# Padded float32 scores, paired latent values and a 128-row decay in a two-layer hybrid decoder

## The chip, the cores and the metric

The kernel runs on one core of one Trainium2 chip. The metric is the device time of one execution in microseconds; smaller is better. All tensors are float32, the sequence has 512 tokens, the model width is 1024.

## The reference

Two layers. Layer 0 mixes tokens by two kinds of attention side by side, layer 1 by two recurrences side by side; after each mixer comes a SwiGLU feed-forward net. What the change touches is this:

```python
# layer 0, latent attention: 8 heads, q and k of 64 + 32 columns, v of 64
o_mla  = softmax(causal(q_mla @ k_mla.T * 96**-0.5)) @ v_mla
# layer 0, differential attention: 4 heads, each with 2 halves of 64 columns
dq, dk = rope(dq), rope(dk)
o2     = softmax(causal(dq @ dk.T * 64**-0.5)) @ dv      # per half, dv has 128 columns
o_diff = rms_norm(o2[half 0] - lam * o2[half 1], subln) * (1 - lambda_init)
# layer 1, state-space group: 8 heads, chunks of 128 tokens
a      = dt * -exp(a_log)
a_cs   = cumsum(a, within the chunk)
seg    = exp(where(causal, a_cs[l] - a_cs[s], -inf))
y_diag = (cc @ bc.T * seg) @ xh
```

## The kernel before, in words

Activations lie feature-major: 128 features on the partitions, 512 tokens in the free dimension. A projection in full precision is split in a high and a low part in a reduced float32 format (`F32R`) and takes three matmuls for each 128 rows of the contraction (`mm3`, L330 to L332). Weights come by SyncE's queue in `wr` tiles (L271) and are split into `wh` and `wl` (L292, L294); pieces 16 to 71 get their lower part on GpSimd, the others on VectorE. At most eight split pieces stand ready (`NSPL`).

Order of work: `attention_layer` first makes the rotary projections of head 0 and the values `dv` of the differential attention; then `weave` runs two generators against each other by hand-written costs: the main one is `diff_attention`, then `latent_attention`, and the filler is all the projections that are left (`diff_projections`, `latent_projections`, `keys`, `queries`, the output projection). The framework under it orders the instructions of each engine and sets the waits. The tiles named `slot` come from one common ring of 37 buffers of 128 x 512, those named `tmp` from one of 10, both are given out again when their last reader is through; PSUM banks `at` are four, `mm` three, `o` one.

Differential attention. `rotary` takes a projection of 128 rows (two halves of 64), turns it (`turn`: two products on VectorE, a sum on GpSimd into `o`) and splits it (`parts`). The queries of a head become three tiles: `t0` and `t1` hold the high part of half 0 and 1 in their own 64 rows and in the other 64 rows a second copy of it; `low` holds what is left. The keys become two tiles: for each half the high part in its own rows and its remainder in the other rows. A score of half c and row block i (`score`, 128 rows, n = 128 (i+1) columns) is then three matmuls: one over 128 rows (L803), the causal mask in bf16 (L804), one over the 64 rows of `low` (L805). `softmax` takes the maximum on VectorE (L708) and the exponential on ScalarE (L710). The two halves are scaled and joined on VectorE (L833, L834) to `p`, which TensorE transposes (L718); the transposes are copied out (L721, L723) and multiplied with `dv` (L821).

Latent attention. The scores are plain float32 matmuls over 128 rows (L701, L702), which the compiler issues as two instructions each, and the mask (L703). The values `v` are four tiles of 128 tokens x 512 columns, 64 columns a head. The product for head h (L867) uses 64 columns of the array and writes PSUM partitions 0 to 63 for an even head, 64 to 127 for an odd one; when both are through, the pair is split once.

State-space group. `ssd` computes dt for 32 columns (four chunks, eight heads), `av` = -dt exp(a_log) (L1073), its running sums as eight rows (`acs`, L1079, L1082), their split, the last sums (L1087, L1091) and their transposes (L1090). In `decay`, for each of eight heads, a row of the selector `sel` spreads one of the eight rows over 128 partitions: two matmuls over 8 rows (L1129, L1131) with the mask between (L1130).

## Time and profile before

| what | value |
|---|---|
| three runs | 1314.17, 1314.99 (median), 1318.85 us |
| profiled execution | 1314.82 us |
| span of its instructions | 1313.0 us |
| TensorE busy | 97% of the span, 6013 matmuls |
| VectorE busy | 56% |
| ScalarE busy | 42% |
| GpSimd busy | 23% |
| mean granted TensorE clock | 0.994 |

The time of the profiled execution is 1.8 us longer than the span from its first to its last instruction. PE is TensorE's matmuls, PEld its weight loads, DVE VectorE, ACT ScalarE, POOL GpSimd, SPq the queue of SyncE. The start of a matmul is measured, its end is modelled, and so neighbouring matmuls overlap in the profile; how long one really holds the engine is read from the distance to the next start. A float32 matmul over full tiles stands in the profile as two instructions. A few matmul records can be missing.

### The profile page before, as it was taken

What the parts mean: (1) busy time and instruction counts of PE and PEld (TensorE: products, weight loads), DVE (VectorE), ACT (ScalarE), POOL (GpSimd) and SP (SyncE); (2) the same over time, 40 slices, a digit from 0 to 9 for tenths busy, and PEclk for the clock granted to TensorE, in tenths of its full rate; (3) what the DMA queues carried; (4) which work ended last, traced back from release to release, by engine and by line L of the source; (5) the groups of instructions that cost most, each with busy time, mean ns of one, the idle gap of its engine ahead of it and who ended that gap; (6) DMA issues with size and microseconds to landing.
All of it is one profiled execution on the core that took longest, in us unless ns stands there. A gap on an engine that the chain in (4) does not pass through costs nothing.

```text
span 1313.0 us, 16410 instructions
## 1 busy us (share of the span) xinstructions
PE 1274.8 (97%) x6013; PEld 1029.9 (78%) x6013; DVE 732.2 (56%) x1330; ACT 545.5 (42%) x1075; POOL 308.2 (23%) x244
## 2 busy tenths in 40 slices
PE   7998889999999999999999999999999999999997
PEld 5766667778888888888888877787788888888886
DVE  6888885557444334444457456799854433344332
ACT  5556554445333223333443463654543322333341
POOL 2524432127222002222100003221322210122212
PEclk9999999999999999999999999999999999999999
DMA  7211211113322333222323321122233223332221
GB/s 236 101 64 33 85 60 49 42 54 112 98 87 82 105 112 97 97 83 89 118 80 97 115 78 33 34 67 62 67 111 97 82 90 118 97 96 87 83 73 64
DMA packets 37135, 112.75 MB, mean 86 GB/s; under 512 B 4272, under 2 KB 10800, under 8 KB 37056
## 3 DMA queue, kind: packets, MB, share of 16 engines
q1 hardware_dynamic: 37056, 111.72, 27.1%
q8 instruction: 47, 0.77, 0.2%
q14 instruction: 32, 0.26, 0.1%
HBM read 109.61 MB, written 2.10 MB: 85 GB/s over the span
## 4 chain that ended last, share of the span: by engine, by line
PE 83%; DVE 10%; ACT 2%; issue 1%; DMA 1%; POOL 1%; SPq 0%; POOLq 0%; DVEq 0%; ACTq 0%
PE mm L330 24%; PE mm L331 24%; PE mm L332 24%; PE o L867 2%; PE at L718 1%; DVE wl L294 1%; PE at L1337 1%; DVE xl L451 1%; PE at L701 1%; DVE nm L708 1%; DMA x<-in_x_dram 0%; PE at L702 0%; DMA par<-in_par_dram 0%; PE at L332 0%; PE at L330 0%
## 5 line engine op out<-in xcount | busy, mean ns | idle before, releaser
L294 DVE TENSOR_TENSOR wl<-wr,wh 128x512 fp32r<-128x512 f32 (+1 forms) x352 | 272.8, 777 | 312.2 <-ACT wh L292 310.1
L292 ACT CAST wh<-wr 128x512 fp32r<-128x512 f32 (+1 forms) x401 | 243.3, 610 | 452.4 <-PE mm L331 398.1
L330 PE MATMUL mm<-xh,wh 128*128 128x512 f32 x944 | 375.7, 398 | 7.1 <-ACT wh L292 6.3
L331 PE MATMUL mm<-xl,wh 128*128 128x512 f32 x944 | 370.9, 393 | 4.2 <-DVE xl L451 4.2
L332 PE MATMUL mm<-xh,wl 128*128 128x512 f32 x944 | 371.2, 393 | 0.0
L330 PEld LDWEIGHTS mm<-xh,wh 128*128 128x128 f32 x944 | 178.8, 189 | 48.4 <-ACT wh L292 6.3
L331 PEld LDWEIGHTS mm<-xl,wh 128*128 128x128 f32 x944 | 178.5, 189 | 42.5 <-DVE xl L451 6.7
L332 PEld LDWEIGHTS mm<-xh,wl 128*128 128x128 f32 x944 | 178.5, 189 | 37.1 <-DVE wl L294 0.4
L929 POOL TENSOR_TENSOR uu<-uu,g 128x512 f32<-128x512 f32 x44 | 70.2, 1598 | 432.8 <-DVE uu L928 408.7
L330 PE MATMUL mm<-hh,wh 128*128 128x512 f32 (+1 forms) x363 | 139.1, 383 | 0.0
L332 PE MATMUL mm<-hh,wl 128*128 128x512 f32 (+1 forms) x363 | 138.9, 383 | 0.0
L331 PE MATMUL mm<-hl,wh 128*128 128x512 f32 (+1 forms) x363 | 138.9, 383 | 0.0
L294 POOL TENSOR_TENSOR wl<-wr,wh 128x512 fp32r<-128x512 f32 (+1 forms) x54 | 70.1, 1303 | 147.4 <-ACT wh L292 147.4
L331 PEld LDWEIGHTS mm<-hl,wh 128*128 128x128 f32 x363 | 68.2, 188 | 13.4
L330 PEld LDWEIGHTS mm<-hh,wh 128*128 128x128 f32 x363 | 68.2, 188 | 13.3
L332 PEld LDWEIGHTS mm<-hh,wl 128*128 128x128 f32 x363 | 68.2, 188 | 13.2
L462 POOL TENSOR_TENSOR acc<-acc,sq 128x512 f32<-128x512 f32 x31 | 45.2, 1457 | 117.4 <-ACT sq L461 116.5
L928 DVE TENSOR_TENSOR uu<-mm,row 128x512 f32<-128x512 f32 x42 | 29.0, 691 | 65.7 <-PE mm L332 65.7
L931 POOL TENSOR_TENSOR hl<-uu,hh 128x512 fp32r<-128x512 f32 x44 | 56.5, 1287 | 29.2 <-ACT hh L930 29.2
L930 ACT CAST hh<-uu 128x512 fp32r<-128x512 f32 x44 | 27.3, 620 | 86.4 <-POOL uu L929 86.4
L710 ACT ACTIVATE p<-at,nm 128x128 f32<-128x128 f32 (+3 forms) x64 | 33.6, 526 | 50.0 <-DVE nm L708 46.5
L954 DVE TENSOR_TENSOR x<-x,mm 128x512 f32<-128x512 f32 x31 | 21.3, 687 | 36.3 <-PE mm L332 36.3
(416 smaller groups left out, 1711.7 us busy)
## 6 DMA issues: line engine op xcount, KB each, us to landing
wr<-in_w_gu_dram SPq DMA_DIRECT2D x88, 512.0 KB, 3.8
wr<-in_w_down_dram SPq DMA_DIRECT2D x32, 512.0 KB, 3.5
wr<-in_w_in_dram SPq DMA_DIRECT2D x20, 512.0 KB, 3.8
wr<-in_w_out_dram SPq DMA_DIRECT2D x12, 512.0 KB, 3.8
wr<-in_w_down_dram SPq DMA_DIRECT2D x32, 192.0 KB, 2.4
wr<-in_w_dv_dram SPq DMA_DIRECT2D x4, 512.0 KB, 4.4
tab<-in_con_dram SPq DMA_DIRECT2D x8, 256.0 KB, 4.3
wr<-in_w_z_dram SPq DMA_DIRECT2D x4, 512.0 KB, 3.6
```

The lines of the kernel that those rows point to most:

```text
L292: nc.scalar.copy(out=hi, in_=raw)
L294: (nc.gpsimd if PL[0] <= self.cut < PL[1] else nc.vector).tensor_tensor(out=lo, in0=raw, in1=hi.bitcast(F32), op=ALU.subtract)
L330: mm(out, lh, rh, start=start, stop=False)
L331: mm(out, lh, rl, start=False, stop=False)
L332: mm(out, ll, rh, start=False, stop=stop)
L462: (nc.vector if fast else nc.gpsimd).tensor_tensor(out=acc, in0=acc, in1=t, op=ALU.add)
L710: nc.scalar.activation(out=pt[:, 0:n], in_=s[:, 0:n], func=AF.Exp, bias=nm, accum_out=rsum)
L867: nc.tensor.matmul(ops[c0 : c0 + 64, vi * P : vi * P + P], self.v[j][:, vh * 64 : (vh + 1) * 64], pT[:, j * P : (j + 1) * P], start=j == 0 ...
L928: nc.vector.tensor_tensor(out=u, in0=pu, in1=row, op=ALU.mult)
L929: nc.gpsimd.tensor_tensor(out=u, in0=u, in1=g, op=ALU.mult)
L930: nc.scalar.copy(out=h, in_=u)
L931: nc.gpsimd.tensor_tensor(out=lo, in0=u, in1=h.bitcast(F32), op=ALU.subtract)
```

## The change

Three edits.

- Differential scores: the keys are no longer split; the sum of `turn` goes straight into a slot. The queries of each half get a tile of their own in plain float32, with zeros in the 64 rows of the other half. A score is one float32 matmul over 128 rows and the mask. A head takes three slots and not five.
- Latent values: `v` is kept in eight tiles. Each holds for two pairs of heads 64 columns of the even head, 64 zeros, 64 columns of the odd head. The product takes two neighbouring groups, so 128 columns: values and zeros for an even head, zeros and values for an odd one, and writes all 128 partitions; both heads of a pair add into the same bank.
- State-space decay: `av` repeats the eight heads sixteen times, so that the running sums, their split, the transposes and the selector all have 128 rows. The selector is loaded with its 128 rows, of which one holds ones.

```diff
--- before.py
+++ after.py
@@ -574,30 +574,26 @@
         u, sw, o = self.tmp("du"), self.tmp("dsw"), self.tmp("dqk")
         nc.scalar.activation(out=u, in_=ps, func=AF.Identity, scale=1.0 if c else 64.0 ** -0.5)
         nc.vector.stream_shuffle(out=sw, in_=u, mask=HALVES)
-
-        t0, t1 = self.slot("d0", F32R), self.slot("d1", F32R)
         a, b = slice(0, 64), slice(64, P)
-        copy, sub = nc.vector.tensor_copy, lambda out, x, hi: nc.vector.tensor_tensor(out=out, in0=x, in1=hi.bitcast(F32), op=ALU.subtract)
 
         def turn():
             nc.vector.tensor_tensor(out=o, in0=u, in1=self.dtab[0], op=ALU.mult)
             nc.vector.tensor_tensor(out=sw, in0=sw, in1=self.dtab[1], op=ALU.mult)
-            nc.gpsimd.tensor_tensor(out=o, in0=o, in1=sw, op=ALU.add)
+            if c:
+                self.dqk[h, 1] = self.slot("dk")
+                nc.gpsimd.tensor_tensor(out=self.dqk[h, 1], in0=o, in1=sw, op=ALU.add)
+            else:
+                nc.gpsimd.tensor_tensor(out=o, in0=o, in1=sw, op=ALU.add)
 
         def parts():
-            nc.scalar.copy(out=t0[a], in_=o[a])
-            nc.scalar.copy(out=t1[b], in_=o[b])
-            if c:
-                sub(t0[b], o[a], t0[a])
-                sub(t1[a], o[b], t1[b])
-                self.dqk[h, 1] = t0, t1
-            else:
-                low = self.slot("dlow", F32R)
-                copy(out=t0[b], in_=o[a])
-                copy(out=t1[a], in_=o[b])
-                sub(low[a], o[a], t0[a])
-                sub(low[b], o[b], t1[b])
-                self.dqk[h, 0] = t0, t1, low
+
+            if c == 0:
+                t0, t1 = self.slot("dq0"), self.slot("dq1")
+                nc.gpsimd.memset(t0[b], 0.0)
+                nc.gpsimd.memset(t1[a], 0.0)
+                nc.scalar.copy(out=t0[a], in_=o[a])
+                nc.scalar.copy(out=t1[b], in_=o[b])
+                self.dqk[h, 0] = t0, t1
 
         self.defer(R0, turn)
         self.defer(R1, parts)
@@ -615,7 +611,11 @@
         ckh, ckl = [self.slot("ckh", F32R) for _ in range(2)], [self.slot("ckl", F32R) for _ in range(2)]
         accq, acck, kr = self.slot("accq"), self.slot("acck"), self.slot("kr")
         self.ck, self.cq = (ckh, ckl), (cqh, cql)
-        self.v = [self.slot("v") for _ in range(4)]
+
+        self.v = [[self.slot("v")[:, 0:384].rearrange("p (g t f) -> p g t f", t=3, f=64) for _ in range(2)] for _ in range(4)]
+        for b in range(NB):
+            for j in range(2):
+                nc.gpsimd.memset(self.v[b][j][:, :, 1, :], 0.0)
         own = {}
 
         def scale_kv():
@@ -664,8 +664,14 @@
                 else:
                     self.square_into(accq, ps, j == 3)
                     self.split(cqh[j - 3], cql[j - 3], ps, par[:, C_QN + j - 3 : C_QN + j - 2])
+
+        def values(b, ps):
+            for j in range(2):
+                src = ps[:, 256 * j : 256 * j + 256].rearrange("p (g t f) -> p g t f", g=2, t=2)
+                nc.scalar.activation(out=self.v[b][j][:, :, 0::2, :], in_=src, func=AF.Identity, scale=own["sk"][:, b : b + 1])
+
         yield from hooked(
-            self.tokmajor4("uv", ckh, ckl, lambda b, ps: nc.scalar.activation(out=self.v[b], in_=ps, func=AF.Identity, scale=own["sk"][:, b : b + 1])),
+            self.tokmajor4("uv", ckh, ckl, values),
             {SQ[0]: scale_q, SQ[1]: spread_q},
         )
         yield from self.keys(0)
@@ -791,18 +797,15 @@
             n = (i + 1) * P
             if t < 16:
                 if i == 0:
-                    yield lambda: (h, 1) in self.dqk
+                    yield lambda: (h, 0) in self.dqk and (h, 1) in self.dqk
                 rs, ri = self.small(2, "rs2", bufs=4), self.small(2, "ri2", bufs=4)
                 pts = []
 
                 def score(c):
                     s = self.bank("at")
-                    hd = slice(64 * c, 64 * c + 64)
-                    qs, ks = self.dqk[h, 0], self.dqk[h, 1]
                     mm = nc.tensor.matmul
-                    mm(s[:, 0:n], qs[c][:, i * P : n], ks[c][:, 0:n], start=True, stop=False)
-                    mm(s[:, i * P : n], self.identb, self.mqb, start=False, stop=False)
-                    mm(s[:, 0:n], qs[2][hd, i * P : n], ks[c][hd, 0:n], start=False, stop=True)
+                    mm(s[:, 0:n], self.dqk[h, 0][c][:, i * P : n], self.dqk[h, 1][:, 0:n], start=True, stop=False)
+                    mm(s[:, i * P : n], self.identb, self.mqb, start=False, stop=True)
                     pts.append(self.softmax(s, n, rs[:, c : c + 1]))
 
                 score(0)
@@ -862,10 +865,16 @@
                 pT, _, vh, vi = lag.pop(0)
                 if vh % 2 == vi == 0:
                     ops = self.bank("o")
-                c0 = vh % 2 * 64
+
+                two = slice(vh % 2, vh % 2 + 2)
                 for j in range(vi + 1):
                     nc.tensor.matmul(
-                        ops[c0 : c0 + 64, vi * P : vi * P + P], self.v[j][:, vh * 64 : (vh + 1) * 64], pT[:, j * P : (j + 1) * P], start=j == 0, stop=j == vi
+                        ops[:, vi * P : vi * P + P],
+                        self.v[j][vh // 4][:, vh // 2 % 2, two, :],
+                        pT[:, j * P : (j + 1) * P],
+                        start=vh % 2 == vi == j == 0,
+                        stop=vh % 2 == 1 and j == vi,
+                        skip_group_check=True,
                     )
                 if vi == 3:
                     del self.q[vh], self.k[vh]
@@ -1068,34 +1077,37 @@
             ts(out=po, in0=po, scalar1=2.0 / k, scalar2=None, op0=ALU.add)
         tt(out=po, in0=po, in1=s1, op=ALU.mult)
         nc.vector.scalar_tensor_tensor(out=dt, in0=z, scalar=0.0, in1=po, op0=ALU.max, op1=ALU.add)
-        ah, av = self.small(8, "ah"), self.small(32, "av")
+        ah, av = self.small(8, "ah"), self.tmp("av")
         nc.scalar.activation(out=ah, in_=par[:, C_ALOG : C_ALOG + 8], func=AF.Exp)
-        nc.vector.scalar_tensor_tensor(
-            out=v32(av), in0=v32(dt), scalar=-1.0, in1=ah.unsqueeze(1).broadcast_to([P, 4, 8]), op0=ALU.mult, op1=ALU.mult
-        )
+        rep16 = lambda t: t.unsqueeze(1).broadcast_to([P, 16, 8])
+        for c in range(4):
+            nc.vector.scalar_tensor_tensor(
+                out=av[:, c * P : (c + 1) * P].rearrange("p (n h) -> p n h", n=16), in0=rep16(v32(dt)[:, c, :]), scalar=-1.0, in1=rep16(ah), op0=ALU.mult, op1=ALU.mult
+            )
 
         ps = self.bank("at")
         for c in range(4):
-            nc.tensor.matmul(ps[0:8, c * P : (c + 1) * P], v32(av)[:, c, :], self.tri, start=True, stop=True)
+            nc.tensor.matmul(ps[:, c * P : (c + 1) * P], av[:, c * P : (c + 1) * P], self.tri, start=True, stop=True)
         yield 850
-        acs = self.slot("acs")[0:8]
-        nc.vector.tensor_copy(out=acs, in_=ps[0:8])
-        acsh, acsl = self.slot("acsh", F32R)[0:8], self.slot("acsl", F32R)[0:8]
+        acs = self.slot("acs")
+        nc.vector.tensor_copy(out=acs, in_=ps)
+        acsh, acsl = self.slot("acsh", F32R), self.slot("acsl", F32R)
         self.split(acsh, acsl, acs)
-        last8 = self.small(32, "last8", rows=8)
+        last8 = self.small(32, "last8")
         for c in range(4):
-            ts(out=v32(last8)[:, c, :], in0=self.ident[0:8, 0:8], scalar1=acs[:, c * P + 127 : c * P + 128], scalar2=None, op0=ALU.mult)
-        ps = self.bank("at")
+            ts(out=v32(last8)[:, c, :], in0=self.ident[:, 0:8], scalar1=acs[:, c * P + 127 : c * P + 128], scalar2=None, op0=ALU.mult)
+        ps, pl = self.bank("at"), self.bank("at")
         for c in range(4):
-            nc.tensor.transpose(ps[:, c * 8 : c * 8 + 8], acs[:, c * P : (c + 1) * P], self.ident[0:8, 0:8])
-        nc.tensor.matmul(ps[:, 64:96], self.ones[0:8, :], last8, start=True, stop=True)
-        yield 300
+            nc.tensor.transpose(ps[:, c * P : (c + 1) * P], acs[:, c * P : (c + 1) * P], self.ident)
+        nc.tensor.matmul(pl[:, 0:32], self.ones, last8, start=True, stop=True)
+        yield 600
+        each = ps.rearrange("p (c h) -> p c h", c=4)[:, :, 0:8]
         nacs, eacs, dec, cdec = (self.small(32, s) for s in ("nacs", "eacs", "dec", "cdec"))
-        ts(out=nacs, in0=ps[:, 0:32], scalar1=-1.0, scalar2=None, op0=ALU.mult)
-        nc.scalar.activation(out=eacs, in_=ps[:, 0:32], func=AF.Exp)
-        tt(out=dec, in0=ps[:, 64:96], in1=nacs, op=ALU.add)
+        ts(out=v32(nacs), in0=each, scalar1=-1.0, scalar2=None, op0=ALU.mult)
+        nc.scalar.activation(out=v32(eacs), in_=each, func=AF.Exp)
+        tt(out=dec, in0=pl[:, 0:32], in1=nacs, op=ALU.add)
         nc.scalar.activation(out=dec, in_=dec, func=AF.Exp)
-        nc.scalar.activation(out=cdec, in_=ps[:, 64:96], func=AF.Exp)
+        nc.scalar.activation(out=cdec, in_=pl[:, 0:32], func=AF.Exp)
         sd = par[:, C_SD : C_SD + 8].unsqueeze(2).broadcast_to([P, 8, 64])
         btok = [self.slot("btok"), self.slot("btok")]
         for g in range(2):
@@ -1114,8 +1126,8 @@
             mts, ys, xdts, xsks, xds, prevs = [], {}, {}, {}, {}, {}
 
             def cb():
-                raw, sel = self.tmp("sel")[0:8], self.tmp("selr", F32R)[0:8]
-                nc.sync.dma_start(out=raw, in_=a["con"][0:8, K_SEL + g * T : K_SEL + (g + 1) * T])
+                raw, sel = self.tmp("sel"), self.tmp("selr", F32R)
+                nc.sync.dma_start(out=raw, in_=a["con"][:, K_SEL + g * T : K_SEL + (g + 1) * T])
                 nc.vector.tensor_copy(out=sel, in_=raw)
                 own["sel"], own["cb"] = sel, self.bank("o")
                 for c in range(4):
```

## Rows read from the trace of the kernel before

**Rows 1.** Busy time by stage: us, then PE, PEld, DVE, ACT, POOL, clock, DMA.
```profile
47.90:190.00 142.10, 128.34 (x604) 96.54 (x602) 116.50 (x250) 83.51 (x215) 59.94 (x46) 0.99 0.23 71
190.00:290.00 100.00, 98.65 (x560) 73.64 (x561) 57.76 (x133) 44.38 (x111) 20.61 (x17) 1.00 0.15 47
755.00:820.00 65.00, 64.75 (x310) 48.08 (x309) 38.89 (x112) 32.74 (x84) 11.72 (x18) 1.00 0.18 56
```

**Rows 2.** Waits of PE, 47.9 to 120 us: total, times, longest.
```profile
PE at L718 <- DVE p L834: 4.7, 3, 3.0
PE o L821 <- DVE pT L723: 1.3, 1, 1.3
PE at L730 <- DVE ot L775: 0.7, 1, 0.7
```

**Rows 3.** PE in order of time, latent attention: start, us, instruction.
```profile
215.17 0.81 PE L701 MATMUL at<-k,q 128*128 128x384 f32 x2
...
216.38 0.40 PE L331 MATMUL mm<-cql,wh 128*128 128x512 f32 x1
216.61 0.40 PE L332 MATMUL mm<-cqh,wl 128*128 128x512 f32 x1
216.94 0.65 PE L867 MATMUL o<-pT,v 128*64 128x128 f32 x4
217.52 0.55 PE L718 MATMUL at<-con,p 128*128 128x128 f32 x3
...
218.14 0.39 PE L331 MATMUL mm<-cql,wh 128*128 128x512 f32 x1
...
218.60 0.38 PE L702 MATMUL at<-k,q 128*128 128x128 f32 x2
...
219.16 0.39 PE L331 MATMUL mm<-dl,wh 128*128 128x512 f32 x1
```

**Rows 4.** PE in order of time, one state-space decay.
```profile
779.12 0.40 PE L332 MATMUL mm<-xh,wl 128*128 128x512 f32 x1
779.45 0.50 PE L1129 MATMUL at<-acsl,selr 8*128 8x512 f32 x1
779.88 0.39 PE L1130 MATMUL at<-msb,identb 128*128 128x512 bf16 x1
...
780.97 0.39 PE L331 MATMUL mm<-xl,wh 128*128 128x512 f32 x1
```

**Rows 5.** PE in order of time, differential scores of 512 and 128 columns.
```profile
131.77 0.40 PE L803 MATMUL at<-d,d 128*128 128x512 f32 x1
...
132.94 0.40 PE L331 MATMUL mm<-xl,wh 128*128 128x512 f32 x1
...
139.95 0.22 PE L803 MATMUL at<-d,d 128*128 128x128 f32 x1
...
140.76 0.39 PE L331 MATMUL mm<-xl,wh 128*128 128x512 f32 x1
```

**Rows 6.** PE in order of time, value products of the differential attention.
```profile
136.04 0.83 PE L821 MATMUL o<-dv,pT 128*128 128x128 f32 x6
...
136.94 0.39 PE L331 MATMUL mm<-xl,wh 128*128 128x512 f32 x1
```

**Rows 7.** Lines of DVE, 20 to 120 us: count, busy us, mean ns, idle before.
```profile
L580 DVE TENSOR_TENSOR d<-dqk,d 64x512 fp32r<-64x512 f32 x8 | 6.5, 807 | 0.4
L596 DVE CAST d<-dqk 64x512 fp32r<-64x512 f32 x4 | 5.9, 1478 | 2.4 <-POOL dqk L585 2.3
...
L580 DVE TENSOR_TENSOR dlow<-dqk,d 64x512 fp32r<-64x512 f32 x8 | 5.5, 686 | 0.2
```

**Rows 8.** DMA issues on the page: count, KB each, us to landing.
```profile
tab<-in_con_dram SPq DMA_DIRECT2D x8, 256.0 KB, 4.3
```

**Rows 9.** DVE and PE in order of time, at PE's longest wait there.
```profile
100.62 2.38 DVE L580 TENSOR_TENSOR d<-dqk,d 64x512 fp32r<-64x512 f32 x2
...
107.38 0.41 PE L718 MATMUL at<-con,p 128*128 128x128 f32 x2 [3.05 <-DVE p L834]
```

## The prediction

> **What bounds the kernel now.** The first view read is the table of stages. In the stretch of the differential attention (47.9 to 190 us) TensorE is busy for 128 of 142 us and VectorE for 117; in the latent attention (190 to 290 us) TensorE is busy for 98.7 of 100 us and VectorE for 58; in the state-space stretch (755 to 820 us) TensorE is busy for 64.8 of 65 us [rows 1]. So TensorE sets the pace in the last two, and in the first it also stands for some 14 us. The second view, who waited for whom, tells for what: up to 120 us TensorE stood for 4.7, 1.3 and 0.7 us, every time for VectorE [rows 2].
>
> A busy TensorE can still be slow, and busy time does not show it, since a matmul's end is modelled. So the third view is the order of time, read by distances between starts. Full-array products of 512 columns start 0.23 us apart (216.38 to 216.61) [rows 3]. Around a matmul that uses part of the array the distances grow. At 779.12 a plain product takes 0.33 us to the start of the 8-row matmul, that one 0.43 to the mask, and L331 starts at 780.97, 1.85 us after the first, for five matmuls of 512 columns that would take 5 x 0.23 = 1.15 at the plain distance [rows 4]. The reader is to see that the instruction before the narrow one, the narrow one and the one after all lose about 0.1 us: the array is emptied when the shape changes, and the next weights are not loaded ahead across the change. All three edits to matmuls remove such changes of shape.
>
> **The change, part by part.** The sum is made against the profiled execution, 1314.8 us (its span of 1313.0 and 1.8 around it); the median of the runs is 1314.99, so nothing has to be shifted.
>
> *Differential scores.* There are 32 of them: four heads, two halves, four widths. Before, each is a full-array matmul in the reduced format, the mask, and a 64-row correction; after, one plain float32 matmul and the mask. From the score's first start to the second product after it, it takes 0.81 us at 128 columns and 1.17 at 512 [rows 5]. What it will take is not a guess: the latent scores already are plain float32 on the full array, with the same mask, and take 0.56 us at 128 columns and 1.21 at 512, to the same point [rows 3]. The float32 matmul itself is dearer, the drains it saves are dearer still at narrow widths. The two middle widths taken on the line between, the four cost 2 x (0.81 + 1.17) = 3.96 us before and 2 x (0.56 + 1.21) = 3.54 after, 0.42 less, eight times: 3.4 us. I take 3, since TensorE also waits in this stretch; the ends are 0 and 3.4.
>
> The Trainium skill has a rule that speaks against this edit: "FP8 and Floating Point Precision", section TensorE Precision Notes, gives true float32 four passes through the array. By that rule alone, an estimate, the 10,240 score columns would go from two passes to four, 10,240 x 2 / 2.4 GHz = 8.5 us more, and the forecast would come out 11.5 us later than mine. The latent scores of this trace carry those passes already in their 1.21 us.
>
> *Latent values.* 80 products (160 instructions) in 32 groups use 128 rows and 64 columns of the array. One group of four: from the product before (216.61) to the second product behind the transposes (218.14) 1.53 us [rows 3]. On the full array, products of the same length with 128-column weights cost (0.90 - 0.23) / 6 = 0.112 us each: six of them and one plain product fill 136.04 to 136.94 [rows 6]. So the same stretch without changes of shape is 0.23 + 4 x 0.112 + 3 x 0.112 + 0.23 = 1.24 us, 0.29 less. Padding adds no instruction, as each already streams 128 columns. 32 x 0.29 = 9.3 us. TensorE bounds this stage, so I take 9. The lower end is 5, if the softmax chain (maximum, exponential, reciprocal, transpose) begins to show when its cover shrinks. The evictions become eight half-width passes of ScalarE in place of four, in a stage where ScalarE is busy for less than half [rows 1]: nothing.
>
> *State-space decay.* Eight decays of three 512-column matmuls. The 1.85 us of [rows 4] become five plain distances, 1.15: 0.70 less, 5.6 us for eight. Some decays follow one another with nothing between and share a drain, so I take 5; the lower end is 3, if VectorE, which takes over behind 820 us, holds the gain back.
>
> Its set-up grows: one VectorE pass over 32 columns becomes four over 128. Their 512 columns cost 0.7 us at the rate of an L580 pass of 512 columns, 2.7 at most if each of the four costs a whole such pass [rows 7]. TensorE waits for them in order. Against it stand the 8-row and 8-column matmuls of the set-up, which lose their drains too, about four changes at 0.1. I enter +0.5 us, ends 0 and 2.7. The selector's two transfers grow from 8 to 128 rows. The nearest row, 256 KB from the same tensor, takes 4.3 us to land [rows 8]; DMA is used to 0.18 in that stretch [rows 1], and the transfer depends on no result, so it can be issued before the decays need it. Nothing, or 4.3 us twice if it is issued only then. Behind it on SyncE's queue stand weight loads, which have buffers of margin.
>
> *VectorE in the rotation.* All its splits go: sixteen L580 passes (6.5 and 5.5 us) and four L596 copies (5.9 us), 17.9 us in all [rows 7]; ScalarE loses eight of its sixteen copies. A quarter, that of head 0, lies before 47.9 us behind the value projection. What the rest is worth is read at TensorE's largest wait: at 100.62 two L580 passes hold VectorE for 2.38 us, the combination p (L834) is queued behind them, and TensorE's transposes stand for 3.05 us until 107.38 [rows 9]. Of the 6.7 us of [rows 2] I take 5: this one and two others at about the same stage. The ends are 0, if the softmax chain's latency is next, and 13.8, if every wait of the stage goes (142.1 - 128.3, [rows 1]). GpSimd gains 16 memsets, in the stretch where it idles for 82 of 142 us [rows 1]: nothing, as long as its adds do not queue behind a slot that is not yet free.
>
> Sum: -3 - 9 - 5 + 0.5 - 5 = -21.5, so 1293 us.
>
> **The rivals.** *The rotation's relief does not come.* The waits move to the next link (maximum, exponential, scale) and only the matmul savings are left: 1314.8 - 16.5 = 1298. For it: waits of the same kind stand after 120 us, where no rotation is left. Against it: the row of 107.38, with split passes straight before it. Chance 0.18.
>
> *The wider weights show.* Each padded value product loads 128 columns of weights and not 64. If the loads came out from behind the products, they would eat the 9: 1302. Against it: the 0.112 us of [rows 6] is paid with 128-column weights. Chance 0.05. The Trainium skill, "TensorE: Matmul & The Clock Gate", section LDWEIGHTS, makes the load's time the column count over 1.2 GHz; by it, an estimate, 64 more columns on 160 loads are 8.5 us, if nothing hides them. The trace's equal distances say that it is hidden.
>
> *No change.* Emptying the array may not be tied to shape but to the change of number format, and stay. For it: each narrow matmul here also has other formats beside it. Against it: [rows 3] change format twice in 0.56 us with hardly a gap. Values and decay then save nothing, the set-up costs its full 2.7, and 3 + 5 - 2.7 = 5.3 are left: 1309.5. Chance 0.05.
>
> *Slower.* The values now take eight slots of the common ring and not four, and GpSimd must clear them before anything is written. If those slots become free only when a head of the differential attention ends, GpSimd stands, and it also makes the lower halves of the weights in this stretch. Eight split pieces ahead, each good for four products of 3 x 0.23, cover 8 x 4 x 0.69 = 22 us. From there TensorE stands: the 21.5 us are gone when GpSimd is held for 43.5 us, and at 55 us the kernel takes 1326. Against it: a head gives up two of its five slots, more than the four added once two heads are in flight. Chance 0.04.
>
> **How the numbers follow.** The forecast as summed has the remaining 0.68. Its own bounds: all gains at their upper ends, 3.4 + 9.3 + 5.6 + 13.8 = 32, give 1283; all at their lower ends, 0 + 5 + 3 + 0 - 2.7, give 1309.5 too. Neither extreme is likely in every term at once; 1285 to 1305 holds the forecast's body and the first two rivals. About 0.5% (6.6 us) is what a measurement here can tell from no change. Faster than 1308.4 are the forecast and the first two rivals, 0.91; no change 0.05; slower 0.04.
>
> **What would show it.** Right: in the profile after, no matmul of the attention or the decay has 64 or 8 rows, or 64 or 8 columns; the value groups stand 0.11 us per instruction with 0.23 before them; a decay takes three distances of 0.23; the score of 512 columns takes about 0.85 us in two halves; the waits of L718 for p before 120 us are short; and the latent stage ends some 17 us earlier. Wrong: GpSimd waiting at the memsets, TensorE waiting for the selector or for av near 762 us, a lowered clock after new gaps, or the drains still there between full-array matmuls.

## The result and the profile after

The changed kernel takes 1293.33 us in the median of four runs (1290.71 to 1297.35), the kernel before 1315.98 (four runs, 1314.17 to 1318.85): ratio 0.983, 95% interval 0.980 to 0.986. The profiled execution took 1293.46 us, its span 1291.7. The head of the page after:

```profile
span 1291.7 us, 16406 instructions
...
PE 1256.4 (97%) x6013; PEld 1032.0 (80%) x6013; DVE 722.9 (56%) x1309; ACT 541.2 (42%) x1071; POOL 314.0 (24%) x260
```

The busy share and the number of matmuls are those of before, and TensorE's busy time is 18.4 us less (1274.8 before); nothing in these lines says where. Positions say it. The stage borders are the first and last starts of one line of TensorE in each trace:

| stretch | before, us | after, us | difference | predicted |
|---|---|---|---|---|
| first score to first latent value product | 47.9 to 191.5 = 143.6 | 47.9 to 184.5 = 136.6 | -7.0 | -8 |
| first to last latent value product | 191.5 to 284.8 = 93.3 | 184.5 to 270.0 = 85.5 | -7.8 | -9 |
| transposes of dt to first transpose of y | 752.1 to 820.4 = 68.3 | 737.1 to 799.8 = 62.7 | -5.6 | -4.5 |
| end of the span | 1313.0 | 1291.7 | -21.3 | -21.5 |

The table of stages, with these borders, before (same columns as [rows 1]):

```profile
47.90:191.50 143.60, 128.93 (x609) 96.97 (x607) 117.59 (x253) 83.51 (x215) 60.06 (x46) 0.99 0.23 74
752.10:820.40 68.30, 68.05 (x326) 50.77 (x325) 40.88 (x117) 35.00 (x87) 12.09 (x19) 1.00 0.18 55
```

and after:

```profile
47.90:184.50 136.60, 124.78 (x604) 94.89 (x603) 107.41 (x229) 78.42 (x207) 63.66 (x60) 0.99 0.24 74
184.50:270.00 85.50, 84.94 (x539) 74.12 (x538) 54.97 (x127) 43.04 (x110) 18.68 (x16) 1.00 0.15 50
737.10:799.80 62.70, 62.56 (x325) 51.16 (x324) 41.74 (x120) 35.00 (x87) 12.08 (x19) 1.00 0.22 68
```

Of the other 0.9 us, 0.7 lies behind the last of these stretches. In the two later ones TensorE is as full as before (92.87 of 93.30 us before in the one of the values) and through sooner. In the first its busy time falls by 4.2 us and its idle time from 14.7 (143.60 - 128.93) to 11.8. The reader keeps this split in mind: busy against idle is what the experiments below turn on. The first border is not at the same work on both sides: of the 24 matmuls of the projection that `weave` runs there (mm<-ckh and mm<-ckl), 16 lie before it in the kernel before and 13 after the change. Three at 0.23 us have moved into the second stretch, so at equal work the first two differences are -6.3 and -8.5.

Busy time also depends on TensorE's granted clock, the column after POOL's. One of the ten-microsecond rows of the kernel before has it below 1:

```profile
150.00:160.00 10.00, 8.22 (x38) 5.99 (x36) 8.41 (x22) 5.91 (x21) 4.61 (x5) 1.00 0.15 52
160.00:170.00 10.00, 8.40 (x34) 6.11 (x33) 7.53 (x15) 6.07 (x14) 2.21 (x3) 0.83 0.32 106
```

Between 164 and 168 us it is at the lower of its two levels, 1.2 and not 2.4 GHz (0.50 from 164.5 to 167.5), and plain products start 0.43 us apart (164.54 to 164.97) and not 0.23. TensorE had stood 1.60 us for VectorE's `ot` until 162.37. Ten microseconds at 0.83 make 1.7 us, an estimate of what the lower level costs there. After the change the same stands between 176 and 180 us, behind a wait of 1.90 us for VectorE's `q`. So both sides of the first row hold one such stretch. The kernels below don't all hold one, and a difference of 1.7 us between two profiles can be this alone. Behind 820 us the trace before holds one more (942 to 946 us) and the trace after none.

TensorE in order of time after, a latent value group (answers [rows 3]):

```profile
208.16 0.39 PE L332 MATMUL mm<-cqh,wl 128*128 128x512 f32 x1
208.39 0.60 PE L871 MATMUL o<-pT,v 128*128 128x128 f32 x4
208.83 0.49 PE L724 MATMUL at<-con,p 128*128 128x128 f32 x3
209.08 0.48 PE L330 MATMUL mm<-cqh,wh 128*128 128x512 f32 x1
209.40 0.39 PE L331 MATMUL mm<-cql,wh 128*128 128x512 f32 x1
```

and a decay (answers [rows 4]):

```profile
763.60 0.39 PE L332 MATMUL mm<-xh,wl 128*128 128x512 f32 x1
763.83 0.40 PE L1141 MATMUL at<-acsl,selr 128*128 128x512 f32 x1
764.07 0.39 PE L1142 MATMUL at<-msb,identb 128*128 128x512 bf16 x1
764.11 0.58 PE L1143 MATMUL at<-acsh,selr 128*128 128x512 f32 x1
764.53 0.39 PE L330 MATMUL mm<-xh,wh 128*128 128x512 f32 x1
764.75 0.40 PE L331 MATMUL mm<-xl,wh 128*128 128x512 f32 x1
```

From L332 to L331 the value group takes 209.40 - 208.16 = 1.24 us, the decay 764.75 - 763.60 = 1.15: both are the predicted distances to the hundredth. The four value instructions take 0.11 us each (208.39 to 208.83), as full-array products do in [rows 6], so the wider weights stay hidden.

A score of 512 columns (answers [rows 5]):

```profile
125.48 1.02 PE L807 MATMUL at<-dk,dq 128*128 128x512 f32 x2
126.33 0.22 PE L808 MATMUL at<-mqb,identb 128*128 128x128 bf16 x1
126.36 0.48 PE L330 MATMUL mm<-xh,wh 128*128 128x512 f32 x1
126.67 0.40 PE L331 MATMUL mm<-xl,wh 128*128 128x512 f32 x1
```

Its two halves take 0.85 us, and 1.19 pass to the second product behind it, against 1.17 of before; at 128 columns the same distance fell from 0.81 to 0.56 (133.73 to 134.29). These, too, are near the latent scores' values of 1.21 and 0.56. Who made TensorE wait up to 120 us (answers [rows 2]):

```profile
PE at L724 <- DVE p L837: 2.9, 3, 1.4
PE o L824 <- DVE pT L729: 0.2, 1, 0.2
```

The 6.7 us of [rows 2] are 3.1, and the longest wait for p is 1.4 us and not 3.0. The link is the same, though: VectorE's p. Behind 120 us it comes back: over the whole first stretch TensorE waits 5.8 us for p after the change and 5.7 before. What shrank is the waiting for `ot` (4.3 to 3.2 us) and for the copies `pT` (3.1 to 0.4). GpSimd does not wait for a slot at its memsets (0.4 us in all before them), and TensorE waits for nothing between 737 and 800 us.

### The profile page after: what moved, and what is told of

Same layout as the page of the kernel before. It is cut to its first block, busy times and chain, and to the rows that moved or that the text cites. A ratio compares the mean times of both kernels' runs of the same rounds, so it can differ in the third digit from the quotient of the medians.

```text
span 1291.7 us, 16406 instructions
## 1 busy us (share of the span) xinstructions
PE 1256.4 (97%) x6013; PEld 1032.0 (80%) x6013; DVE 722.9 (56%) x1309; ACT 541.2 (42%) x1071; POOL 314.0 (24%) x260
## 4 chain that ended last, share of the span: by engine, by line
PE 87%; DVE 8%; ACT 2%; issue 1%; DMA 0%; POOL 0%; SPq 0%; POOLq 0%; DVEq 0%; ACTq 0%
PE mm L330 25%; PE mm L331 25%; PE mm L332 25%; PE o L871 1%; PE at L724 1%; PE at L1349 1%; PE at L707 1%; DVE p L837 1%; DVE xl L451 1%; PE at L708 1%; PE at L807 1%; DMA x<-in_x_dram 0%; PE at L332 0%; PE at L330 0%; PE at L331 0%
## 5 line engine op out<-in xcount | busy, mean ns | idle before, releaser
L331 PE MATMUL mm<-xl,wh 128*128 128x512 f32 x944 | 370.6, 393 | 4.3 <-DVE xl L451 4.2
L332 PE MATMUL mm<-xh,wl 128*128 128x512 f32 x944 | 370.2, 392 | 0.0
L331 PEld LDWEIGHTS mm<-xl,wh 128*128 128x128 f32 x944 | 178.3, 189 | 42.6 <-DVE xl L451 7.4
L332 PEld LDWEIGHTS mm<-xh,wl 128*128 128x128 f32 x944 | 178.2, 189 | 37.1 <-DVE wl L294 0.2
L332 PE MATMUL mm<-hh,wl 128*128 128x512 f32 (+1 forms) x363 | 138.9, 383 | 0.0
L331 PE MATMUL mm<-hl,wh 128*128 128x512 f32 (+1 forms) x363 | 138.9, 383 | 0.0
L331 PEld LDWEIGHTS mm<-hl,wh 128*128 128x128 f32 x363 | 68.2, 188 | 13.4
L332 PEld LDWEIGHTS mm<-hh,wl 128*128 128x128 f32 x363 | 68.2, 188 | 13.3
L963 DVE TENSOR_TENSOR x<-x,mm 128x512 f32<-128x512 f32 x31 | 21.3, 688 | 36.5 <-PE mm L332 36.5
```

The lines of the kernel that those rows point to most:

```text
L331: mm(out, lh, rl, start=False, stop=False)
L332: mm(out, ll, rh, start=False, stop=stop)
L963: nc.vector.tensor_tensor(out=self.x[:, m, :], in0=self.x[:, m, :], in1=ps, op=ALU.add)
```

## Experiments

The theory: a change of the array's shape costs TensorE about 0.1 us before, in and after the narrow matmul; removing it is worth the distances above, and the differential attention gains both from that and from VectorE's relief. Rival theories: the price belongs to the number format; the differential part's gain is all relief, or none of it. Every kernel below was timed in five rounds beside the kernel before, which took 1315.19 to 1316.27 us in the three sittings. The changed kernel was not timed again, and differences against it are taken against its 1293.33.

**One edit alone, three kernels.** Each is the kernel before with one of the three edits of the diff, whole.

> The kernel before with the differential edit alone (padded float32 scores, no splits of the rotation). Theory (the gain adds up from changes of array shape taken away and from a lighter VectorE): 7 us less than before, ratio 0.9945; the last product with dv starts near 170 us and everything behind it is moved by that amount without change. Rival (the edits share one cause, so one alone buys little): under 3 us, ratio above 0.9975. Rival (the scores alone lengthen, the rest made up for it): ratio above 1.

> The kernel before with the latent values padded to 128 columns alone. Theory: 8 us less, ratio 0.994; from the first latent value product to the last about 85.5 us in place of 93.3. Rival (wider weights show, and the stage is shortened by something else): under 2 us.

> The kernel before with the state-space edit alone (128 rows in the decay and its set-up). Theory: 5 to 6 us less, ratio 0.9955 to 0.996, all of it between 752 and 820 us. Rival (the work of VectorE behind 820 us absorbs it): under 3 us.

The kernel before took 1315.74 us beside them.

| edit | us | ratio, interval | difference | its own stretch |
|---|---|---|---|---|
| differential scores | 1307.84 | 0.994 (0.992 to 0.995) | -7.9 | 143.6 to 135.9 |
| latent values | 1308.08 | 0.994 (0.993 to 0.995) | -7.7 | 93.3 to 85.4 |
| decay | 1308.37 | 0.995 (0.993 to 0.996) | -7.4 | 68.3 to 62.7 |

The three add up to 23.0, the whole change gave 22.7: within the intervals, some 2 us each way for one edit, no edit eats into another. The decay's own stretch gives 5.6 of its 7.4; its trace is already 2.4 us early at 749.7 us, before anything that it changes (752.1 before), and so the stretch is taken as its worth. Of these 2.4 us, 1.7 are the clock: up to there this execution has no stretch like that of 164 to 168 us before.

**VectorE's passes put back.** The changed kernel, and VectorE again makes sixteen differences and eight copies of 64 x 512, into a tile that nobody reads. The scores stay as changed.

```diff
+            dj, x = self.dj, self.dqk[h, 1] if c else o
+            sub = lambda out, in0, in1: nc.vector.tensor_tensor(out=out, in0=in0, in1=in1, op=ALU.subtract)
+            if c:
+                sub(dj[b], x[a], x[a])
+                sub(dj[a], x[b], x[b])
...
+                nc.vector.tensor_copy(out=dj[b], in_=o[a])
+                nc.vector.tensor_copy(out=dj[a], in_=o[b])
+                sub(dj[a], o[a], t0[a])
+                sub(dj[b], o[b], t1[b])
```

> The changed kernel with the removed VectorE passes of the rotation put back into a tile that nothing reads: sixteen differences and eight copies of 64 x 512, the same count and shapes as before; the scores stay padded float32. The eight ScalarE casts stay out. Theory (about 4 us of the differential part are VectorE's relief, about 3 the scores): 4 us more than the changed kernel, near 1297, ratio to before 0.986, with waits of TensorE on p before 120 us grown by 3 to 5 us. Rival (the relief is worth nothing, the scores alone shorten the stage): within 1 us of the changed kernel, 1293. Rival (nearly all is relief): 7 us more, 1300.

1303.44 us (1301.12 to 1306.59), ratio 0.991 (0.989 to 0.992): 10.1 us slower than the changed kernel, more than 3 us beyond the largest value expected. The profiled execution, the fastest of the five, is 7.7 us slower than the changed kernel's. Its table of stages from 47.9 us to the first latent value product (here and below the window starts at 47.9 us; the first score itself starts between 47.4 and 49.1 unless said):

```profile
47.90:191.70 143.80, 125.13 (x601) 94.31 (x601) 119.23 (x251) 77.22 (x206) 64.11 (x60) 0.99 0.22 71
```

TensorE's busy time is that of the changed kernel (125.1 against 124.8), its idle time is 18.7 and not 11.8, and the stretch is as long as before the change (it holds one stretch at the lower clock, as those of the kernel before and the changed kernel do). With VectorE's load back, the whole gain of this stretch is gone, though every score is still the cheap one.

**The other half: the kernel before without the splits.** Its scores keep their three matmuls; VectorE's splits and copies become zeros from GpSimd. So the scores are those of rounded queries and keys, without the remainders.

```diff
             if c:
-                sub(t0[b], o[a], t0[a])
-                sub(t1[a], o[b], t1[b])
+                nc.gpsimd.memset(t0[b].bitcast(F32), 0.0)
+                nc.gpsimd.memset(t1[a].bitcast(F32), 0.0)
...
-                copy(out=t0[b], in_=o[a])
-                copy(out=t1[a], in_=o[b])
-                sub(low[a], o[a], t0[a])
-                sub(low[b], o[b], t1[b])
+                nc.gpsimd.memset(t0[b].bitcast(F32), 0.0)
+                nc.gpsimd.memset(t1[a].bitcast(F32), 0.0)
+                nc.gpsimd.memset(low.bitcast(F32), 0.0)
```

> The kernel before with the three-term scores in their old shapes, but without VectorE's splits of queries and keys: their remainders and second copies are set to zero by GpSimd, so the scores are those of the rounded queries and keys. Only the relief of VectorE is left of the differential edit. Theory as predicted: 4 to 5 us less than before, 1310 to 1311. Theory as the last run suggests: 8 to 9 us less, 1306 to 1307, with the waits of TensorE on p before 120 us gone from 4.7 to under 2 us.

1308.34 us (1307.05 to 1309.75), ratio 0.994 (0.993 to 0.996), the kernel before 1316.27 beside it: -7.9, as much as the whole differential edit. Its table of stages for the same stretch:

```profile
47.90:184.00 136.10, 126.47 (x606) 95.82 (x604) 105.08 (x233) 84.34 (x217) 66.73 (x61) 1.00 0.25 78
```

and that of the differential edit alone:

```profile
47.90:183.80 135.90, 124.25 (x609) 94.48 (x607) 106.75 (x231) 78.60 (x206) 62.00 (x52) 1.00 0.25 78
```

The cheaper scores save 2.2 us of busy time (126.47 to 124.25), and TensorE's idle time is 2.0 longer (9.63 to 11.65). Neither window holds a stretch at the lower clock. Taken from each kernel's own first score (47.7 and 48.3 us) the stretches are 136.3 and 135.5 us long. Most of what the scores give, the next wait takes.

**Scores over 64 rows.** The changed kernel, each score a plain float32 matmul over the 64 rows of its half.

```diff
-                    mm(s[:, 0:n], self.dqk[h, 0][c][:, i * P : n], self.dqk[h, 1][:, 0:n], start=True, stop=False)
+                    hd = slice(64 * c, 64 * c + 64)
+                    mm(s[:, 0:n], self.dqk[h, 0][c][hd, i * P : n], self.dqk[h, 1][hd, 0:n], start=True, stop=False)
```

> The changed kernel with each differential score taken over the 64 rows of its half in place of 128 rows with zeros; the same plain float32 matmul, the same number of passes, tiles and clears. Theory (the price is the change of array shape): the distances around each score grow by about 0.3 us, 32 times, 9 to 10 us on TensorE, of which part falls into waits that are there anyway: 5 to 9 us more than the changed kernel, 1298 to 1302. Rival (the price is the change of number format): no more than 1 us, 1293 to 1294.

1300.6 us (1300.13 to 1301.8), ratio 0.988 (0.987 to 0.990): 7.3 us slower than the changed kernel. TensorE in order of time:

```profile
128.69 0.39 PE L332 MATMUL mm<-xh,wl 128*128 128x512 f32 x1
129.00 1.12 PE L808 MATMUL at<-dk,dq 64*128 64x512 f32 x2
130.06 0.23 PE L809 MATMUL at<-mqb,identb 128*128 128x128 bf16 x1
130.10 0.48 PE L330 MATMUL mm<-xh,wh 128*128 128x512 f32 x1
130.41 0.40 PE L331 MATMUL mm<-xl,wh 128*128 128x512 f32 x1
```

Format, columns and number of matmuls are those of the changed kernel, only the rows differ. From L332 to L331 it takes 1.72 us; over 128 rows it is 0.23 + 1.19 = 1.42. The 0.3 us are paid before the score (0.31 against 0.23) and in it (1.06 to the mask against 0.85). Thirty-two times 0.3 is 9.6; the stretch's busy time grew by 8.9 and its idle time fell by 2.8. The price belongs to the shape, not to the format.

**The decay over 64 rows.** The changed kernel, the decay's matmuls over the first 64 of the 128 rows, the selected row among them.

```diff
-                nc.tensor.matmul(ps, one, acsl, start=True, stop=False)
+                nc.tensor.matmul(ps, one[0:64], acsl[0:64], start=True, stop=False)
...
-                nc.tensor.matmul(ps, one, acsh, start=False, stop=True)
+                nc.tensor.matmul(ps, one[0:64], acsh[0:64], start=False, stop=True)
```

> The changed kernel with the two matmuls of each decay over the first 64 rows, which hold the selected row, in place of 128. Theory (any part of the array costs the same change of shape, 64 rows as 8): each decay takes 0.70 us more, 5 to 5.6 us in all, 1298 to 1299. Rival (only very narrow matmuls cost): under 1.5 us, 1293 to 1295.

1298.89 us (1297.91 to 1302.29), ratio 0.988 (0.986 to 0.989): 5.6 us slower than the changed kernel. TensorE in order of time:

```profile
766.37 0.40 PE L332 MATMUL mm<-xh,wl 128*128 128x512 f32 x1
766.70 0.49 PE L1141 MATMUL at<-acsl,selr 64*128 64x512 f32 x1
767.12 0.39 PE L1142 MATMUL at<-msb,identb 128*128 128x512 bf16 x1
767.44 0.50 PE L1143 MATMUL at<-acsh,selr 64*128 64x512 f32 x1
767.87 0.50 PE L330 MATMUL mm<-xh,wh 128*128 128x512 f32 x1
768.21 0.40 PE L331 MATMUL mm<-xl,wh 128*128 128x512 f32 x1
```

1.84 us, as the 8 rows of [rows 4] with 1.85: half of the array costs what a sixteenth does. Of the three widths tried, only 128 rows are free.

**Three reduced-format terms, padded, with and without the splits.** Can the score be cheaper still? The changed kernel with the scores of before, but the remainder of each half in a tile of its own with zeros in the other rows, so that all three matmuls use 128 rows. First with all of VectorE's splits back:

```diff
...
-                    mm(s[:, 0:n], self.dqk[h, 0][c][:, i * P : n], self.dqk[h, 1][:, 0:n], start=True, stop=False)
-                    mm(s[:, i * P : n], self.identb, self.mqb, start=False, stop=True)
+                    mm(s[:, 0:n], qs[c][:, i * P : n], ks[c][:, 0:n], start=True, stop=False)
+                    mm(s[:, i * P : n], self.identb, self.mqb, start=False, stop=False)
+                    mm(s[:, 0:n], qs[2 + c][:, i * P : n], ks[c][:, 0:n], start=False, stop=True)
```

> The changed kernel with the three-term scores of before, but the remainder of the queries padded with zeros to 128 rows, a tile for each half: no change of shape and no float32 passes, and all VectorE splits of before back, eight more clears on GpSimd than before the change. Theory as predicted (scores 3, relief 5): TensorE gains about 0.25 us a score against plain float32 and the relief is lost, near 1291 to 1294. Theory as the last run suggests (the stage is bound by VectorE's splits, their removal is worth 8 to 9 us and a faster score nothing): 1300 to 1303.

Then the same with GpSimd's zeros in place of the splits and copies (the remainders are left out of the scores again):

> The changed kernel with three-term scores over padded tiles (no change of shape, two passes a column in place of four) and VectorE's splits left out: remainders and second copies are zeros from GpSimd, so the scores are those of the rounded queries and keys. It tells what a faster score is worth once VectorE is relieved. Theory as predicted (TensorE's time in this stage counts): 5 to 7 us less than the changed kernel, 1286 to 1288. Theory as the runs suggest (the chain through VectorE sets this stage, a faster score only lengthens the waits): within 2 us, 1291 to 1294.

With the splits 1301.4 us (1299.15 to 1301.81), ratio 0.989 (0.987 to 0.990): 8.1 slower than the changed kernel. Without them 1293.14 (1289.99 to 1294.86), ratio 0.983 (0.981 to 0.985): the same as the changed kernel. Table of stages with the splits:

```profile
47.90:191.50 143.60, 123.50 (x616) 95.81 (x615) 119.53 (x254) 83.90 (x219) 65.51 (x60) 0.98 0.23 74
```

and without:

```profile
47.90:181.00 133.10, 118.17 (x608) 92.35 (x608) 107.42 (x230) 81.79 (x215) 68.29 (x72) 1.00 0.25 80
```

With VectorE at 119.5 us TensorE's busy time is the lowest but one and the stretch as long as before the change; it holds two stretches at the lower clock and not one (92 to 97 and 109 to 114 us, behind waits of 2.3 and 3.3 us for VectorE), which is 1.7 us of it. Without the splits TensorE is busy 6.6 us less than in the changed kernel (124.78 to 118.17), 1.7 of it because the clock does not fall. In this profiled execution, the fastest of its runs, 3.1 us come back as idle time, and the median shows none of the rest.

**More relief.** The changed kernel, the second product of the rotation on GpSimd.

```diff
-            nc.vector.tensor_tensor(out=sw, in0=sw, in1=self.dtab[1], op=ALU.mult)
+            nc.gpsimd.tensor_tensor(out=sw, in0=sw, in1=self.dtab[1], op=ALU.mult)
```

> The changed kernel with the second product of the rotation (the turned half by the sine table, eight passes of 128 x 512) on GpSimd in place of VectorE. Theory (VectorE's passes before 120 us are what the differential stage pays for): VectorE loses 7 us, at the rate of the last runs (8 us of time for 20 us of passes) 2 to 3 us less, 1290 to 1291. Rival (the relief has reached its end, the softmax chain is next): within 1 us, 1293. Rival (GpSimd's products come late and the rotation is ready too late): 1295 or more.

1294.53 us (1293.47 to 1294.88), ratio 0.984 (0.982 to 0.985): no gain. The first latent value product starts where it did (184.3 us against 184.5), but the first score starts at 50.9 us and not at 47.9. From there the stretch is 133.4 us long, 3.2 us shorter than the changed kernel's 136.6, and 1.7 of that is the clock, which doesn't fall here. Of the 3.0 us lost ahead of it, 1.0 is a wait of TensorE for ScalarE's `dv` (L548) that the changed kernel doesn't have. So this product on GpSimd gains nothing; that relief as such has reached its end is not shown.

**The same idea in another place.** In the gated recurrence two of the levels, 32 and 64, use 32 and 64 columns of the array. The changed kernel, with full 128-column weights there; the extra results go to PSUM and aren't read.

```diff
...
-                    for b in blocks:
-                        t = c * P + b
-                        nc.tensor.matmul(part[b : b + m, c, :], ks[:, t : t + m], qs[:, t + m : t + 2 * m], start=True, stop=True)
+                    odd = bl(qs, m)[:, c * (64 // m) : (c + 1) * (64 // m), 1, :]
+                    nc.tensor.matmul(part[:, c, :], ks[:, c * P : (c + 1) * P], odd, start=True, stop=True)
...
```

> The changed kernel with the two narrow levels of the gated recurrence (blocks of 32 and 64 tokens) taken with 128 weight columns like the other levels: 24 instructions a head become 16, no change of array shape is left there, and the copies read the same blocks out of a wider result. Theory (a change of shape costs TensorE about 0.3 us around each group, 8 groups): 2 to 2.5 us on TensorE; of it 1.5 to 2.5 us reach the end, 1291 to 1292. Rival (the stretch behind 820 us is VectorE's): within 0.5 us of the changed kernel, 1293.

And together with the product on GpSimd:

> Both of the last two edits on the changed kernel. If they add up: the sum of both differences, near 1289; if the moved product does not pay, the time of the run with the gated recurrence alone.

1297.2 us (1295.11 to 1298.94), ratio 0.986 (0.984 to 0.988), and both together 1296.65 (1294.53 to 1298.98), ratio 0.986 (0.984 to 0.988). Not faster: the medians lie 3.9 and 3.3 us above the changed kernel, where of the first a gain was expected and at worst no change. In the profile the stretch that holds the levels (first transpose of y to the last product with the state, L1384 and here L1382) is 101.4 us long, against 98.2; another 2.2 us of this execution lie ahead of it, 1.7 of them one more stretch at the lower clock (57 to 62 us). A group of level 32 in the changed kernel, first TensorE and then its weight loads in order of time:

```profile
868.89 0.40 PE L330 MATMUL mm<-yh,wh 128*128 128x512 f32 x1
869.22 0.45 PE L1341 MATMUL at<-qs,ks 128*32 128x32 f32 x16
869.60 0.50 PE L331 MATMUL mm<-yl,wh 128*128 128x512 f32 x1
869.93 0.39 PE L332 MATMUL mm<-yh,wl 128*128 128x512 f32 x1
```

```profile
869.22 0.33 PEld L1341 LDWEIGHTS at<-qs,ks 128*32 128x32 f32 x16 [0.37 <-DVE wl L294]
```

and the same two views with the full array:

```profile
871.19 0.40 PE L330 MATMUL mm<-yh,wh 128*128 128x512 f32 x1
871.43 1.00 PE L1339 MATMUL at<-qs,ks 128*128 128x64 f32 x8
872.24 0.47 PE L331 MATMUL mm<-yl,wh 128*128 128x512 f32 x1
872.55 0.39 PE L332 MATMUL mm<-yh,wl 128*128 128x512 f32 x1
```

```profile
871.20 1.09 PEld L1339 LDWEIGHTS at<-qs,ks 128*128 128x128 f32 x8
```

The change of shape does go: 0.24 us ahead of the group where 0.33 were, 0.31 behind it where 0.33 were. But the eight full products take 0.81 us, 0.10 each, where sixteen narrow ones take 0.38. Eight loads of 128 columns stand over 1.09 us, sixteen of 32 over 0.33. Products that stream 128 columns take 0.11 each on the full array [rows 6], and streaming only 64 hardly shortens that, so the time here is put down to the load. The Trainium skill, "TensorE: Matmul & The Clock Gate", section on LDWEIGHTS, makes a load's time its columns over 1.2 GHz, an estimate of 0.107 us for 128 columns; the 0.10 us of the trace are near it. The whole group is 1.36 against 1.04 us, that of level 64 1.35 (893.83 to 895.18) against 1.27 (870.86 to 872.13): 0.4 for a head, 1.6 for the four. The named waits of the levels make up the rest: with the full array

```profile
PE at L1347 <- DVE ks L1353: 1.4, 2, 0.9
PE at L1339 <- DVE qs L1353: 1.2, 2, 0.6
...
PE o L1380 <- ACT sc L1341: 0.5, 1, 0.5
```

are 3.1 us between 795 and 910 us; in the changed kernel the waits for VectorE's ks and qs stand for 1.4 and the last one is not there.

## Why the prediction was right

The forecast was 1293, and 1293.33 came; the mechanism held, and errors in the sizes cancelled.

**What bounds the kernel.** Right. TensorE sets the pace in the latent and the state-space stretches: what was taken from it there came out at the end, as far as the intervals tell. In the differential attention VectorE's chain holds TensorE up, and the experiments show it more strongly than the prediction put it.

**Latent values, 9 predicted, 7.8 measured (8.5 at equal work; 7.7 by themselves).** With the scores the stage ends 14.8 us earlier (284.8 to 270.0) where some 17 were forecast. The group of four saves the predicted 0.29 us exactly. Read in the same way, the groups of two save 0.30 (1.20 to 0.90), those of eight 0.29 (1.75 to 1.46), some behind a score 0.23 (2.45 to 2.22); a group of six whose transposes wait for VectorE saves 0.01 (2.33 to 2.32). The term took the best case 32 times; some 0.3 us more fall outside the borders, which leave out the entry of the first group and the exit of the last.

**Decay, 5 predicted, 5.6 measured with its set-up.** The distances are those predicted. From the first decay to the transposes of y it is 40.95 us before (779.45 to 820.4) and 35.97 after (763.83 to 799.8), 5.0 less. The set-up was entered as 0.5 more and came out 0.6 less: from the transposes of dt to the first decay 27.35 us before and 26.73 after. Neither its four passes nor the selector's transfer shows: TensorE is idle for 0.14 us in the whole stretch (62.70 - 62.56). The drains of its own small matmuls went too.

**Differential scores, 3 predicted, and VectorE's relief, 5 predicted.** Here two terms were mis-sized. Relief alone, with the old matmuls, gives 7.9; the scores on top of it give at most 0.8 us of the stretch and nothing that the times can tell. The step that failed is the one that took the score's distances, 3.4 us, as a saving on the end, with 0.4 off for TensorE's waits, and read the relief off TensorE's waits up to 120 us. The saving of the matmuls is there (2.2 us of busy time), but it lies in a stage in which the chain through VectorE keeps time, and 2.0 of it turn into idle time. The relief was worth more than the waits of [rows 2], since VectorE's passes also push the softmax behind them; of the 14.7 us in which TensorE is idle 5.0 went without the splits (14.67 to 9.63), and the busy time fell by 2.5, of which 1.7 are the stretch at the lower clock that this execution doesn't have. How often the clock falls over many executions differs less: its mean is 0.9945 in the six of the kernel without splits and 0.9936 in the eleven of the kernel before beside them, an estimate of 1 us of the 7.9. Whether it falls less because TensorE waits less is not shown. So the sum of the two, 8, met 7.9 by accident: one term was 3 too high and the other 3 too low. The relief's upper bound of 13.8 held it.

That does not make the padding idle. Had the scores become float32 on 64 rows, the end would have been 7.3 us later; the padding is what lets the splits go at no price with the scores kept whole.

Two readings behind the relief were short. VectorE lost eight copies and not four: [rows 7] has those of L596 alone, and the four of L597 take another 1.7 us. And at the row of 107.38 the two L580 passes are through at 103.0; nearer to p stands the copy L596, from 104.20 to 105.65, which the reading of [rows 9] left out.

**The rivals.** *Relief does not come*: refuted by the splits left out (-7.9) and by the passes put back (+10.1). *Wider weights show*: refuted for products that stream 128 columns, by the 0.11 us between them; the full-array levels of the recurrence show what it looks like where 64 are streamed. *Format, not shape*: refuted by the two kernels with 64 rows. *Slots*: GpSimd never stood for them, although two heads in flight give up four slots, as many as are added and not more.

**The rule against it.** The Trainium skill, "FP8 and Floating Point Precision", section TensorE Precision Notes, gives true float32 four passes. The trace agrees on the passes: a score of 512 columns takes 0.85 us, a reduced-format product of the same size 0.23. The forecast by that rule alone, 11.5 us later, did not come: padded three-term scores with VectorE relieved, whose two matmuls of 0.23 us stand against 0.85, take 1293.14 against 1293.33.

**What stays open.** Why the latent stage at equal work gained 8.5 us in the whole change and 7.2 alone (there 19 of the 24 matmuls lie before the border); how much of the relief is the clock; and whether the fastest scores are worth a microsecond or two, which the spread of their runs (1289.99 to 1294.86) hides.

## What to carry to other kernels

Read a small matmul's price from the distance between its neighbours' starts on both sides, not from its busy time; where it uses part of the array, see what zeros that fill the array would cost, and count the weight load against the columns that are streamed: at 128 streamed columns a 128-column load was hidden, at 64 the products took as long as the load, and the narrow products with their change of shape were the cheaper ones (1.04 against 1.36 us). Before a saving on the bounding engine is entered in a sum, look whether that engine also stands in the stage; if it does, most of the saving can go to the next wait (2.0 of 2.2 us of busy time here), and the chain it waits for is where the time is to be had. The other way it does not hold: of some 9.6 us added by scores over 64 rows, 7.3 came out. Before two profiles are compared by a few microseconds, read the granted clock by stage, since one stretch at the lower level was 1.7 us here. Where an edit moves both at once, undo each by itself, since a right sum can be made of two wrong terms.

## What the runs showed that was not expected

Narrow matmuls can be cheaper than full ones even with the change of shape around them: sixteen of 32 columns in 0.38 us against eight of the full array in 0.81, for the same useful results. And half of the array costs as much as a sixteenth of it: the decay takes 1.84 us over 64 rows, 1.85 over 8, 1.15 over 128.

VectorE's copies of 64 x 512 took 1.48 us each in L596 [rows 7], twice its subtractions of the same size, but 0.42 in L597, of the same form. The trace before shows what differs, GpSimd and VectorE in order of time:

```profile
102.41 2.96 POOL L294 TENSOR_TENSOR wl<-wr,wh 128x512 fp32r<-128x512 f32 x2
104.20 1.45 DVE L596 CAST d<-dqk 64x512 fp32r<-64x512 f32 x1
107.26 0.42 DVE L597 CAST d<-dqk 64x512 fp32r<-64x512 f32 x1
```

Each of the four L596 runs beside a GpSimd pass and ends 0.28 us behind it (here 105.65 against 105.37), and each of the four L597 finds GpSimd idle. Rounding is not the reason: with plain float32 as the output (passes put back) the two copies take 1.46 and 0.50 us. So part of what the relief took from VectorE was time beside GpSimd's passes, some 1.06 us four times; that the pass holds the copy up is how the rows look, and no run tries it.
